# Two feature tiles of the expert stage lent to the weight stream as a ninth place

## The chip, the cores and the metric

The kernel runs on one core of a Trainium2 chip. The metric is the device time of one execution in microseconds (us). TensorE (PE) does the matmuls, ScalarE (ACT) and VectorE (DVE) do what stands between them, GpSimd (POOL) does little, and SyncE (SP) issues nearly all DMAs of weights from HBM into on-chip memory (SBUF).

## The reference, cut to what matters

Two layers over 256 tokens of width 1024. The even layer ends in a dense SwiGLU, the odd one in eight experts, of which each token uses two. Nearly three quarters of the time go into the experts:

```python
def swiglu(x, w_gate, w_up, w_down):
    return (jax.nn.silu(x @ w_gate) * (x @ w_up)) @ w_down

def moe_swiglu(x, router, w_gate, w_up, w_down):
    ...
    logits = (t @ router).astype(jnp.float32)
    top_logits, top_idx = lax.top_k(logits, TOP_K)
    ...
    for e in range(N_EXPERTS):
        out = out + gates[:, e:e + 1] * swiglu(t, w_gate[e], w_up[e], w_down[e])
    return out.reshape(bsz, s, d)
...
        x = layer_norm(ALPHA * x + moe_swiglu(x, router, w_gate, w_up, w_down), ln2_g, ln2_b)
```

Each expert has a gate and an up matrix of 1024 x 3584 and a down matrix of 3584 x 1024, all float32.

## The kernel before

**The pieces.** The experts' weights are 336 MB-sized pieces (`chunks`, filled by `expert`), here numbered 0 to 335 in the order in which they are used. `raw_half` gives each piece a place in SBUF (tile name `raw`) and issues its DMA at once (L136, 1 MB). A place is one of eight in the ring of the pool `rawp` (`RAW_BUFS`), or, for pieces 0 to 59, one of the extra places of `AHEAD`: fixed tiles of the pool `fx` (tags ft, fd, fa, ... f1) that stand empty for a while; each is open for a span of pieces. Which piece gets which place is worked out ahead of the program: a loop goes through the pieces and gives each the open place whose last piece is the oldest (`held_by`, result in `ahead`). A piece given a place waits until the place's last reader has read it.

**The order of work.** All DMAs of pieces are issued on SP's queue, in the order of the pieces. SP's queue is in order: while one DMA waits for its place, the ones behind it are not issued. What a piece waits for is a semaphore of PE or DVE, whichever read the old content last. A program-ordered plan (`plan`) lists, for every expert p and block of features f (`FBLOCKS`: 1024, 1024, 1024, 512), a gate item "g", an up item "u" and a down item "d"; a block of 1024 is four pieces. Experts are handled in places 0, 2, 6, 1, 4, 5, 3, 7, of which two or three overlap (`STARTS`). The items' instructions stand in this order on every engine.

**Wide and narrow experts.** `CAPS` gives the token slots of an expert. Blocks of 64 or 32 slots use the piece as it landed (PE reads `raw`). Experts 2, 1 and 3, in that order, have a 128-slot block: each half of a piece is first copied by ACT (`whi`, L154), then DVE makes the remainder (`wlo`, L161), and PE multiplies with both. Up to 6 `whi` and 5 `wlo` halves exist. Expert 1 has a block of 32 slots besides.

**The feature tiles.** The picked tokens of a 128-slot block (names `xgw`, `xgw2`, read by PE as `xgw`) lie in a tile of 128 x 8 x 256, the size of a piece. There are two in turn (`picked`): the pool `fx` has one under the tag f0 (experts 2 and 3), the pool `mop` one under the tag xgw (expert 1). Expert 0's 64-slot features (`xg`) use xgw as well, and at the very end the gains and biases of the last layer norm (`lnf`, 2 DMAs of 512 KB on POOL's queue, L1613) go into it. A block's features are picked by PE with a one-hot matrix S, made on DVE (L1214), and are last read by the last up matmul of their expert.

**Other names that come up.** `fdk` (L1339, L1352) are silu and product of a block, `mh` its transposed copy, `acc` the down accumulators. L1535 is a branch (`tc.If`) which all engines pass at about 1218 to 1234 us; SP reaches it after it has issued pieces up to 319, and goes on with piece 320 (a down piece of expert 3) behind it. L1655 and L1656 apply `lnf` in the last 5 us of work.

Of the kernel before, what the change touches and what calls it, by code (L numbers as in the profile page):

```python
# [8 lines left out]
F32 = mybir.dt.float32  # L9
# [8 lines left out]
P = 128  # L18
# [21 lines left out]
AHEAD = {"ft": (0, 50), "fd": (20, 24), "fa": (2, 17), "fc": (3, 48), "fe": (7, 50), "fb": (8, 56), "f0": (9, 16), "f1": (10, 60)}  # L40

IN_HI, IN_LO = (15, 16, 17), (18, 19)
# [18 lines left out]
FBLOCKS = ((0, 1024), (1024, 1024), (2048, 1024), (3072, 512))  # L61
# [17 lines left out]
def tile_trunk(ctx: ExitStack, tc: tile.TileContext, a: dict, out: bass.AP, caps=CAPS, starts=STARTS,  # L79
# [17 lines left out]
    def bank(tag="mm"):  # L97
        return psum.tile([P, 512], F32, name=tag, tag=tag)
# [5 lines left out]
    chunks, slot_pools = [], {"ra": rawp}  # L104
    raws, his, los, ahead = {}, {}, {}, {}
# [11 lines left out]
    def raw_half(n):  # L117

        c, h = divmod(n, 2)
        src, k, f = chunks[c]  # L120
        if c in ahead and ahead[c] in ("whi", "wlo"):
            if c not in raws:
                pool = hip if ahead[c] == "whi" else lop
                raws[c] = [pool.tile([P, k // 2, f], F32, name=ahead[c]) for _ in range(2)]
                for i, r in enumerate(raws[c]):
                    sy.dma_start(r, src()[:, i * k // 2:(i + 1) * k // 2, :])
            return raws[c][h]
        if c not in raws:
            tag = ahead.get(c, "raw")
            raws[c] = slot_pools[tag[:2]].tile([P, k, f], F32, name="raw", tag=tag)  # L130
            v = src()
            if c < FIRST_CUT:
                for i in range(2):
                    sy.dma_start(raws[c][:, :, i * P:(i + 1) * P], v[:, :, i * P:(i + 1) * P])
            elif c < len(chunks) - LAST_CUT:
                sy.dma_start(raws[c], v)  # L136
            else:
                for i in range(2):
                    sy.dma_start(raws[c][:, i * k // 2:(i + 1) * k // 2, :], v[:, i * k // 2:(i + 1) * k // 2, :])
        return raws[c][:, :, h * P:(h + 1) * P] if k == DB else raws[c][:, h * k // 2:(h + 1) * k // 2, :]  # L140
# [5 lines left out]
    def prep(hi_to, lo_to):  # L146
        hi_to, lo_to = (min(v, 2 * len(chunks) - 1) for v in (hi_to, lo_to))
        while made["hi"] <= hi_to:
            n = made["hi"]
            made["hi"] += 1  # L150
            r = raw_half(n)
            if n not in his and n not in plain:
                his[n] = hip.tile(list(r.shape), F32R, name="whi")
                se.activation(his[n], r, AF.Copy)  # L154
        while made["lo"] <= lo_to:
            n = made["lo"]
            made["lo"] += 1
            if n not in los and n not in plain:
                r = raw_half(n)
                los[n] = lop.tile(list(r.shape), F32R, name="wlo")  # L160
                ve.tensor_tensor(los[n], r, his[n].bitcast(F32), op=OP.subtract)  # L161
# [7 lines left out]
    def hold(n):  # L169

        r = raw_half(n)
        for d in (his, los):
            if n not in d:
                d[n] = spare_half().rearrange("p (k f) -> p k f", k=r.shape[1])
                if d is his:
                    se.activation(his[n], r, AF.Copy)
                else:
                    ve.tensor_tensor(los[n], r, his[n].bitcast(F32), op=OP.subtract)

    def use(count=1):  # L180

        n = state["use"]
        state["use"] = n + count
        if count == 1:
            end = n > 2 * len(chunks) - TAIL
            prep(n + (TAIL_HI if end else LOOK_HI), n + (TAIL_LO if end else LOOK_LO))
            return his.get(n), los.get(n)
        prep(n + count, n + count - 1)
        return [(his[m], los[m]) for m in range(n, n + count)]
# [38 lines left out]
    n_moe = 2 * len(chunks)  # L228
    NFB = len(FBLOCKS)

    held_by = {"raw": [-1] * 8}
    held_by.update({tag: [-2] for tag in AHEAD})
    for c in range(max(c1 for _, c1 in AHEAD.values())):
        if c in IN_HI + IN_LO:
            continue
        tag = min((v[0], t) for t, v in held_by.items() if t == "raw" or AHEAD[t][0] <= c < AHEAD[t][1])[1]
        held_by[tag] = held_by[tag][1:] + [c]  # L240
        if tag != "raw":
            ahead[n_moe // 2 + c] = tag
    passes = [[(p, n - n0) for p, n0 in starts if 0 <= n - n0 < NFB] for n in range(max(n0 for _, n0 in starts) + NFB)]
    plan = []
    for n, g in enumerate(passes):
# [8 lines left out]
    for p, n0 in sorted(starts, key=lambda s: s[1]):  # L254
        kept = [(m, k) for m, k in kept if m + NFB > n0]
        spills[p] = []
        for _, n in _blocks(caps[p]):
            k = 2 if n == P else 1
# [3 lines left out]
    if len(passes[-1]) == 1 and caps[last] < P:  # L262

        plan.insert(len(plan) - 2, plan.pop(len(plan) - 5))

    def expert(p, w, r0, nr, c0, ncol):
        def src():
            if p and p not in eid_reg:
                eid_reg[p] = sy.value_load(ctli[0:1, p:p + 1], min_val=0, max_val=NE - 1)
            if p == 0:  # L270
                v = w[0, r0:r0 + nr, c0:c0 + ncol]
            else:
                v = w[bass.ds(eid_reg[p], 1), r0:r0 + nr, c0:c0 + ncol].rearrange("o r f -> (o r) f")
            return v.rearrange("(k p) f -> p k f", p=P)
        chunks.append((src, nr // P, ncol))

    for what, p, f in plan:
        f0, nf = FBLOCKS[f]
# [121 lines left out]
    def ws_tile(w, xT, b=None, t=None):  # L400


        wh, wl = w
        if b is None:
            b = bank()
        o, ol = b, b[:, :T]
        if t is not None:
            o = ol = b.rearrange("p (s u f) -> p s u f", s=2, u=2)[:, :, t, :]
        for k in range(DB):
            x_, xl = xT[:, k, :], xT[:, k, :T]  # L410
            if t is not None:
                x_ = xl = x_.rearrange("p (s u f) -> p s u f", s=2, u=2)[:, :, t, :]
            if k < DB - 1:
                mm(o, wh[:, k, :], x_, k == 0, False)
                mm(ol, wl[:, k, :], xl, False, False)
            else:
                mm(ol, wl[:, k, :], xl, False, False)
                mm(o, wh[:, k, :], x_, False, True)
        return b
# [3 lines left out]
    def combine(b, o=None):  # L423
        c = evac[0][:, 1024 + T * (evac[1] % 2):][:, 0:T]
        se.activation(c, b[:, T:], AF.Copy)
        if o is None:
            o = evac[0][:, T * (evac[1] % 4):][:, 0:T]
        evac[1] += 1
        ve.tensor_tensor(o, b[:, :T], c, op=OP.add)
        return o  # L430
# [230 lines left out]
    def ws3(w):  # L661

        b = bank()
        for k in range(DB):
            mm(b[:, :T], w[0][:, k, :], xT[:, k, :T], k == 0, False)
            mm(b[:, :T], w[0][:, k, :], xT[:, k, T:], False, False)
        for k in range(DB):
            mm(b[:, :T], w[1][:, k, :], xT[:, k, :T], False, k == DB - 1)
        return b[:, :T]
# [42 lines left out]
    for pair in range(2):  # L712
        for h in range(2):
            s = ws3(use())
# [14 lines left out]
    for q in range(4):  # L729
        w = use_plain() if PLAIN_B else use()  # L730
        for t in range(2):
            for j in range(2):
                k = 2 * q + j
# [118 lines left out]
    first, firsts = [], []  # L852
# [22 lines left out]
    for i in range(1, NFP):  # L875
# [4 lines left out]
        b = [ws_tile(use(), x1T) for _ in range(2)]  # L880
# [30 lines left out]
    first, firsts = [], []  # L911
# [26 lines left out]
    b = bank()  # L938
# [6 lines left out]
    for pair in range(2):  # L945
        for h in range(2):
            w = use()
            j = 2 * pair + h
            s = combine(ws_tile(w, x2T))
# [7 lines left out]
    for n in range(2):  # L957
        b = bank()
        for h in range(4):
            mm(b[:, h * P:(h + 1) * P], vd[:, n, h * P:(h + 1) * P], swT[:, h, :], True, True)  # L960
        s = fc[:, 3, :]
# [7 lines left out]
    for pair in range(2):  # L969
        for h in range(2):  # L970
            w = use()
            j = 2 * pair + h
            s = combine(ws_tile(w, x2T))
# [7 lines left out]
    for pair in range(2):  # L981
        for h in range(2):
            w = use()
            j = 2 * pair + h
            s = combine(ws_tile(w, x2T))
# [68 lines left out]
    b = bank()  # L1054
# [21 lines left out]


    mop = ctx.enter_context(tc.tile_pool(name="mop", bufs=2, reuse_waits="tile"))
    events = {}
    clock = {"n": 0, "free": 0, "banks": 0}  # L1080

# [425 lines left out]
    at = len(plan)  # L1507
    for n, p in sorted([(plan.index(("g", p, 0)), p) for p, n0 in starts if n0], reverse=True):
        at = min(at, n - 1)
# [104 lines left out]
    for bi in range(len(blocks[last])):  # L1614
        if spills[last][bi]:
            spilled(last, NFB - 1, bi, macc[last, bi])
        else:
            n = len(macc[last, bi])
            ysum[last, bi] = [row0(i) for i in range(n)]
            if n == 1:  # L1620
                y, b = ysum[last, bi][0], macc[last, bi][0]
# [66 lines left out]
```

## Time and profile before

| | us |
|---|---|
| median of 3 runs | 1293.33 (1292.98 to 1293.68) |
| the profiled execution, its own time | 1298.7 |
| its span | 1297.0 |
| PE busy in it | 1248.3 (96%) |
| DVE busy / ACT busy | 711.9 / 515.4 |
| weights and the rest moved by DMA | 421.02 MB |
| pieces of 1 MB for the experts, issued on SP | 336 |

PE is busy nearly all the time, and so are the DMA engines in the last two thirds. With two resources so full, the rows to read are PE's few gaps and what ended each, and the stretches in which the DMA engines stand idle and what the next issue waited for. The clock of TensorE is in the rows as the granted share of full speed: 1.00 is 2.4 GHz, 0.50 is 1.2 GHz.

### The profile page before, as it was taken

What the parts mean: (1) busy time and instruction counts of PE and PEld (TensorE: products, weight loads), DVE (VectorE), ACT (ScalarE), POOL (GpSimd) and SP (SyncE); (2) the same over time, 40 slices, a digit from 0 to 9 for tenths busy, and PEclk for the clock granted to TensorE, in tenths of its full rate; (3) what the DMA queues carried; (4) which work ended last, traced back from release to release, by engine and by line L of the source; (5) the groups of instructions that cost most, each with busy time, mean ns of one, the idle gap of its engine ahead of it and who ended that gap; (6) DMA issues with size and microseconds to landing.
All of it is one profiled execution on the core that took longest, in us unless ns stands there. A gap on an engine that the chain in (4) does not pass through costs nothing. (4 is left out here: it accounts for less than half of the span.)

```text
span 1297.0 us, 17004 instructions
## 1 busy us (share of the span) xinstructions
PE 1248.3 (96%) x6433; PEld 803.9 (62%) x6433; DVE 711.9 (55%) x1066; ACT 515.4 (40%) x705; POOL 32.1 (2%) x69
## 2 busy tenths in 40 slices
PE   7989999999999999999999999999999999999795
PEld 7848888888876466855654455554454556765341
DVE  5997676667985247665234533534333575575233
ACT  4246555546432245554234332332221445454110
POOL 4000000001000001000000000000000000000000
PEclk9999999999999999999989999999999999999898
DMA  8425755176878999999969999899999999999995
GB/s 293 172 70 174 256 185 194 58 249 195 331 266 338 378 406 406 350 358 405 387 240 401 388 401 402 344 364 404 391 402 408 409 405 404 400 403 405 390 352 201
DMA packets 146642, 421.02 MB, mean 325 GB/s; under 512 B 6816, under 2 KB 43368, under 8 KB 146552
## 3 DMA queue, kind: packets, MB, share of 16 engines
q1 hardware_dynamic: 145048, 414.58, 84.0%
q0 software_dynamic: 1504, 5.28, 1.2%
q8 instruction: 52, 0.85, 0.3%
q14 instruction: 38, 0.31, 0.1%
HBM read 418.78 MB, written 1.05 MB: 324 GB/s over the span
## 5 line engine op out<-in xcount | busy, mean ns | idle before, releaser
L161 DVE TENSOR_TENSOR wlo<-raw,whi 128x1024 fp32r<-128x1024 f32 x354 | 419.1, 1225 | 200.8 <-ACT whi L154 169.8
L154 ACT ACTIVATE whi<-raw 128x1024 fp32r<-128x1024 f32 x354 | 357.6, 1052 | 218.3 <-DMA raw<-in_odd_moe_w_up 83.6
L101 PE MATMUL mm<-whi,xgw 128*128 128x512 f32 x672 | 216.6, 404 | 3.0 <-DVE total L1504 2.0
L101 PEld LDWEIGHTS mm<-whi,xgw 128*128 128x128 f32 x672 | 124.4, 191 | 48.1 <-issue 11.1
L101 PE MATMUL mm<-wlo,xgw 128*128 128x512 f32 x336 | 133.3, 397 | 0.5 <-DVE wlo L161 0.5
L101 PE MATMUL mm<-raw,f1k 128*64 128x512 f32 (+3 forms) x768 | 131.8, 552 | 0.0
L101 PE MATMUL mm<-big,whi 128*128 128x512 f32 (+1 forms) x448 | 129.7, 368 | 1.6 <-ACT whi L154 1.6
L101 PE MATMUL acc<-whi,mh 128*128 128x512 f32 (+1 forms) x352 | 111.7, 410 | 0.6 <-ACT whi L154 0.6
L101 PE MATMUL mm<-raw,fek 128*64 128x512 f32 (+1 forms) x512 | 103.3, 551 | 6.6 <-DVEq L1535 6.6
L101 PE MATMUL mm<-big,wlo 128*128 128x256 f32 x384 | 93.1, 284 | 0.0
L101 PE MATMUL acc<-raw,fbs 128*64 128x512 f32 (+1 forms) x560 | 91.5, 513 | 0.5 <-DMA raw<-in_odd_moe_w_down 0.5
L101 PEld LDWEIGHTS mm<-big,whi 128*128 128x128 f32 x448 | 75.5, 194 | 13.1 <-ACT whi L154 2.0
L101 PEld LDWEIGHTS mm<-raw,f1k 128*64 128x64 f32 (+1 forms) x768 | 40.6, 127 | 67.2 <-issue 59.9
L101 PEld LDWEIGHTS acc<-whi,mh 128*128 128x128 f32 (+1 forms) x352 | 62.5, 186 | 27.2 <-ACT whi L154 7.4
L101 PEld LDWEIGHTS mm<-raw,fek 128*64 128x64 f32 x512 | 35.3, 138 | 63.8 <-issue 58.7
L101 PEld LDWEIGHTS mm<-wlo,xgw 128*128 128x128 f32 x336 | 64.0, 191 | 15.5 <-DVE wlo L161 1.0
L1339 ACT ACTIVATE fdk<-mm 128x512 f32<-128x512 f32 (+1 forms) x37 | 21.1, 572 | 127.4 <-PE mm L101 126.7
L101 PEld LDWEIGHTS mm<-big,wlo 128*128 128x128 f32 x384 | 69.1, 191 | 3.6
L101 PE MATMUL acc<-wlo,mh 128*128 128x512 f32 (+1 forms) x184 | 70.2, 413 | 0.5 <-DVE wlo L161 0.5
L101 PEld LDWEIGHTS acc<-raw,fbs 128*64 128x64 f32 (+1 forms) x560 | 28.3, 125 | 53.2 <-issue 46.1
L1352 DVE TENSOR_TENSOR fdk<-mm,fdk 128x512 f32<-128x512 f32 (+1 forms) x37 | 24.4, 662 | 66.7 <-PE mm L101 66.7
L101 PE MATMUL acc<-whi,ffh 128*128 128x512 f32 x176 | 54.9, 393 | 0.0
(289 smaller groups left out, 1271.8 us busy)
## 6 DMA issues: line engine op xcount, KB each, us to landing
raw<-in_odd_moe_w_gate SPq DMA_DIRECT2D x112, 1024.0 KB, 11.5
raw<-in_odd_moe_w_up SPq DMA_DIRECT2D x111, 1024.0 KB, 11.4
raw<-in_odd_moe_w_down SPq DMA_DIRECT2D x106, 1024.0 KB, 11.9
raw<-in_even_ffn_w_gate SPq DMA_DIRECT2D x11, 1024.0 KB, 6.5
raw<-in_even_ffn_w_up SPq DMA_DIRECT2D x11, 1024.0 KB, 8.5
raw<-in_even_ffn_w_down SPq DMA_DIRECT2D x11, 1024.0 KB, 6.8
raw<-in_odd_w_in SPq DMA_DIRECT2D x10, 1024.0 KB, 14.7
raw<-in_even_w_in SPq DMA_DIRECT2D x5, 1024.0 KB, 9.0
```

The lines of the kernel that those rows point to most:

```text
L101: te.matmul(o, lhsT, rhs, start=start, stop=stop)
L154: se.activation(his[n], r, AF.Copy)
L161: ve.tensor_tensor(los[n], r, his[n].bitcast(F32), op=OP.subtract)
L1339: se.activation(s[:, n * i:n * (i + 1)], v, AF.Silu)
L1352: ve.tensor_tensor(s[:, c], v, s[:, c], op=OP.mult)
```

## The change

No computation is added or removed, and no engine's instructions change their order. What changes is the place of some pieces, and with it what they and the pieces behind them wait for. The loop over `held_by` moves behind the making of `plan` and goes through all pieces. Two tags get additional spans, worked out from the plan, in which they are open for pieces:

- xgw from piece 59 to 87 (after expert 0's last up item, until shortly before expert 1's features are picked): pieces 59, 68, 77, 86 get it;
- f0 from piece 101 to 219 (after expert 2's last up item, until shortly before expert 3's features are picked): 101, 110, ... 218;
- xgw again from 223 to 333 (after expert 1's last up item): 223, 232, ... 331.

Within a span the pieces go through nine places in turn, not eight, so that each one but the first takes the place of the piece nine before it. The first piece of a span takes a place that was a feature tile until then.

```diff
-            raws[c] = slot_pools[tag[:2]].tile([P, k, f], F32, name="raw", tag=tag)
+            raws[c] = slot_pools[tag[:2]].tile([P, k, f], F32, name="raw", tag=tag, **({"bufs": 1} if tag == "xgw" else {}))
...
-    for c in range(max(c1 for _, c1 in AHEAD.values())):
-        if c in IN_HI + IN_LO:
-            continue
-        tag = min((v[0], t) for t, v in held_by.items() if t == "raw" or AHEAD[t][0] <= c < AHEAD[t][1])[1]
...
+    at, spans = 0, {}
+    for item in plan:
+        spans[item] = at
+        at += FBLOCKS[item[2]][1] // 256
+    wides = [(p, n0) for p, n0 in sorted(starts, key=lambda s: s[1]) if caps[p] >= P]
+    free = {"f0": [], "xg": []}
+    firsts = {p: spans["g", p, 0] for p, _ in starts}
+    lasts = {p: spans["u", p, NFB - 1] + 2 for p, _ in starts}
+    free["f0"].append((lasts[wides[0][0]] + 3, firsts[wides[2][0]] - 10))
+    free["xg"].append((lasts[0] + 3, firsts[wides[1][0]] - 14))
+    free["xg"].append((lasts[wides[1][0]] + 3, at - 2))
+
+    def open_at(tag, c):
+        return tag in AHEAD and AHEAD[tag][0] <= c < AHEAD[tag][1] or any(a <= c < b for a, b in free.get(tag, ()))
+
+    held_by.setdefault("xg", [-2])
+    for c in range(at):
+        if c in IN_HI + IN_LO:
+            continue
+        tag = min((v[0], t) for t, v in held_by.items() if t == "raw" or open_at(t, c))[1]
+        held_by[tag] = held_by[tag][1:] + [c]
+        if tag != "raw":
+            ahead[n_moe // 2 + c] = {"xg": "xgw"}.get(tag, tag)
...
+    slot_pools["xg"] = mop
```

SP's queue at the start of the f0 span. The first row is piece 101 (expert 6, up), the next are pieces 102 to 104 (expert 1, gate), 105 and 106; a wait on PE_49 or DVE_49 is the wait for the place, DMAHW is the queue's own:

```order
 L136 DMA raw_5287<-in_odd_moe_w_up 128x2x1024 [waits DMAHW3_49,PE_49]
...
-L136 DMA raw_5301<-in_odd_moe_w_gate 128x2x1024 [waits DMAHW4_49,PE_49]
...
-L136 DMA raw_5322<-in_odd_moe_w_gate 128x2x1024 [waits DMAHW5_49,PE_49]
...
-L136 DMA raw_5340<-in_odd_moe_w_gate 128x2x1024 [waits DMAHW6_49,DVE_49]
...
+L136 DMA raw_5301<-in_odd_moe_w_gate 128x2x1024 [waits DMAHW4_49]
...
+L136 DMA raw_5322<-in_odd_moe_w_gate 128x2x1024 [waits DMAHW5_49]
...
+L136 DMA raw_5340<-in_odd_moe_w_gate 128x2x1024 [waits DMAHW6_49]
...
 L136 DMA raw_5388<-in_odd_moe_w_gate 128x2x1024 [waits DMAHW7_49,DVE_49]
...
-L136 DMA raw_5424<-in_odd_moe_w_gate 128x2x1024 [waits DMAHW0_49,PE_49]
...
+L136 DMA raw_5424<-in_odd_moe_w_gate 128x2x1024 [waits DMAHW0_49,DVE_49]
```

Nothing moved in place; the three pieces behind 101 have no wait for a place of their own any more, because 101's wait, in front of them, is for a later event than theirs would be. Pieces 60 (behind 59) and 224 to 227 (behind 223) lose theirs in the same way.

DVE's queue at the same place, the same before and after (the names raw_5301, raw_5322 and raw_5340 are pieces 102, 103 and 104):

```order
L441 TENSOR_TENSOR mh_5298<-mm_5291,mh_5298 128x4x128 [waits Activation_49]
L161 TENSOR_TENSOR wlo_5318<-raw_5301,whi_5312 128x1024 [waits DMAHW4_49,DVE_49,Activation_49]
L161 TENSOR_TENSOR wlo_5326<-raw_5301,whi_5316 128x1024 [waits DVE_49,Activation_49]
L161 TENSOR_TENSOR wlo_5332<-raw_5322,whi_5324 128x1024 [waits DMAHW5_49,DVE_49,Activation_49]
L1352 TENSOR_TENSOR fdk_4046<-mm_5281,fdk_4046 128x512 [waits PE_49]
L1214 TENSOR_SCALAR S_5337<-slot0_64_3355,valsP_3671 128x128 x2
L161 TENSOR_TENSOR wlo_5344<-raw_5322,whi_5330 128x1024 [waits DVE_49,Activation_49]
```

Nothing moved here: S for the picking of a block stands behind three remainders, of pieces 102 and 103.

POOL's queue at its end. The third span gives xgw to piece 331 last, so `lnf` waits behind it; in before it waits for expert 1's features:

```order
-L1613 DMA lnf<-in_odd_ln_g 128x1024 [waits DMASW3_49,DVE_49,PE_49]
-L1613 DMA lnf<-in_odd_ln_b 128x1024 [waits DMASW4_49]
...
+L1554 UNCONDITIONAL_BRANCH
+L1632 DMA lnf<-in_odd_ln_g 128x1024 [waits DMAHW3_49,DMAHW2_49,DMAHW4_49,DMAHW1_49,DMAHW5_49,DMAHW0_49,DMAHW6_49,DMASW3_49,DMAHW7_49,DVE_49,PE_49]
+L1632 DMA lnf<-in_odd_ln_b 128x1024 [waits DMASW4_49]
```

The two loads stand where they stood, and wait for the last reading of piece 331, and for hardware DMA queues besides.

## Rows read from the trace of the kernel before

**Rows 1.** The page, section 1: busy time by engine.

```profile
PE 1248.3 (96%) x6433; PEld 803.9 (62%) x6433; DVE 711.9 (55%) x1066; ACT 515.4 (40%) x705; POOL 32.1 (2%) x69
```

**Rows 2.** Stretches: length, busy by engine (count), granted clock, DMA share, GB/s.

```profile
840.00:850.00 10.00, 10.00 (x54) 5.59 (x52) 0.68 (x1) 2.34 (x5) 0.00 (x0) 1.00 0.67 218
950.00:960.00 10.00, 10.00 (x56) 5.86 (x57) 0.00 (x0) 0.00 (x0) 0.00 (x0) 1.00 1.03 410
654.40:661.20 6.80, 6.80 (x26) 4.44 (x26) 1.55 (x2) 0.64 (x2) 0.00 (x0) 0.50 0.89 313
1005.95:1009.36 3.41, 3.41 (x10) 2.63 (x9) 3.00 (x4) 3.34 (x5) 0.00 (x0) 0.50 1.03 410
1220.99:1227.80 6.81, 3.22 (x8) 1.12 (x10) 0.00 (x0) 0.00 (x0) 0.00 (x0) 0.50 1.02 396
```

**Rows 3.** Timeline of SP: start, length, issue of pieces 59 and 101.

```profile
512.65 0.37 SPq L136 DMA_DIRECT2D raw<-in_odd_moe_w_up  x1
630.85 0.37 SPq L136 DMA_DIRECT2D raw<-in_odd_moe_w_up  x1
```

**Rows 4.** Timeline of PE and ACT, 523 to 542 us; in brackets idle time and releaser.

```profile
523.93 3.67 PE L101 MATMUL mm<-raw,xg 128*64 128x256 f32 x32
531.25 1.05 ACT L154 ACTIVATE whi<-raw 128x1024 fp32r<-128x1024 f32 x1
541.33 1.06 ACT L154 ACTIVATE whi<-raw 128x1024 fp32r<-128x1024 f32 x1 [0.29 <-PE mm L101]
```

**Rows 5.** Timeline of PE, ACT and DVE, 643 to 654 us.

```profile
643.66 0.39 PE L101 MATMUL mm<-wlo,xgw 128*128 128x512 f32 x1
648.12 5.78 ACT L154 ACTIVATE whi<-raw 128x1024 fp32r<-128x1024 f32 x6
649.20 3.50 DVE L161 TENSOR_TENSOR wlo<-raw,whi 128x1024 fp32r<-128x1024 f32 x3 [0.25 <-ACT whi L154]
652.61 0.68 DVE L1352 TENSOR_TENSOR fdk<-mm,fdk 128x512 f32<-128x512 f32 x1
653.21 0.47 DVE L1214 TENSOR_SCALAR S<-slot,valsP 128x128 f32<-128x128 f32 x2
653.63 2.97 PE L101 MATMUL mm<-S,tok 128*128 128x64 f32 x16 [1.61 <-DVE S L1214]
```

**Rows 6.** Timeline of PE and ACT: expert 1's last up matmul, expert 3's first gate pieces.

```profile
976.90 0.40 PE L101 MATMUL mm<-wlo,xgw 128*128 128x512 f32 x1
1002.69 2.00 ACT L154 ACTIVATE whi<-raw 128x1024 fp32r<-128x1024 f32 x2 [10.65 <-DMA raw<-in_odd_moe_w_gate]
1003.80 0.73 PE L101 MATMUL mm<-whi,xgw 128*128 128x512 f32 x2 [0.99 <-ACT whi L154]
1005.06 0.50 PE L101 MATMUL mm<-wlo,xgw 128*128 128x512 f32 x1 [0.53 <-DVE wlo L161]
```

**Rows 7.** Timeline of PE behind the branch.

```profile
1224.58 15.54 PE L101 MATMUL mm<-raw,fek 128*64 128x512 f32 x64 [6.64 <-DVEq L1535]
1240.70 0.74 PE L101 MATMUL acc<-whi,mh 128*128 128x512 f32 x2 [0.58 <-ACT whi L154]
1241.96 0.50 PE L101 MATMUL acc<-wlo,mh 128*128 128x512 f32 x1 [0.52 <-DVE wlo L161]
```

**Rows 8.** The chain that ended last: start, length, what.

```profile
1234.38 5.12 DMA raw<-in_odd_moe_w_down
1239.59 1.06 ACT whi L154
1248.28 15.97 DMA raw<-in_odd_moe_w_down
1272.28 8.76 PE acc L101 x40
```

**Rows 9.** The tile lnf: its readers, its issue and the time to landing.

```profile
L1655 DVE SCALAR_TENSOR_TENSOR total<-total,ln_y,lnf x4: 743/746/752, 1288.1 to 1292.3; 128x512 f32<-128x512 f32 x4
L1613 POOL DMA_DIRECT2D lnf<-in_odd_ln_g x1: 585/585/585, 977.6 to 977.6; - x1
DMA to landing us min/median/max: 7.9/9.0/10.0
```

More of the change, by code (lines that the diff above doesn't have):

```diff
@@ L229, in tile_trunk @@
     NFB = len(FBLOCKS)
-    held_by = {"raw": [-1] * 8}
-    held_by.update({tag: [-2] for tag in AHEAD})
-    for c in range(max(c1 for _, c1 in AHEAD.values())):
-        if c in IN_HI + IN_LO:
-            continue
-        tag = min((v[0], t) for t, v in held_by.items() if t == "raw" or AHEAD[t][0] <= c < AHEAD[t][1])[1]
-        held_by[tag] = held_by[tag][1:] + [c]
-        if tag != "raw":
-            ahead[n_moe // 2 + c] = tag
     passes = [[(p, n - n0) for p, n0 in starts if 0 <= n - n0 < NFB] for n in range(max(n0 for _, n0 in starts) + NFB)]
@@ L264, in tile_trunk @@
         plan.insert(len(plan) - 2, plan.pop(len(plan) - 5))
+    held_by = {"raw": [-1] * 8}
+    held_by.update({tag: [-2] for tag in AHEAD})
+    at, spans = 0, {}
[19 more added lines that the diff above has]
+            ahead[n_moe // 2 + c] = {"xg": "xgw"}.get(tag, tag)
     def expert(p, w, r0, nr, c0, ncol):
```

## The prediction

> **What bounds the kernel now.** I read the page first. PE is busy for 96% of the span [rows 1], so in the expert part a change of waits can win only what PE still idles, plus what low clock those idle times bring. Then the stretches by clock and DMA: where the stream of pieces runs freely the DMA engines are full, 410 GB/s at a share of 1.03 [rows 2], and a piece of 1.05 MB takes 1.05/0.410 = 2.56 us. At 840 to 850 us the share is 0.67: all places are taken there and the DMA engines wait for PE [rows 2]. So the two are nearly level: PE sets the pace over long stretches, and the stream is late at single points.
>
> Last, PE's gaps in its timeline, with what ended each. Three could depend on weights. At 652.02 PE waits 1.61 us for S [rows 5], and then runs at half clock (0.50, 1.2 GHz) from 654.40 to 661.20 [rows 2]. At 1002.8 and 1004.5 it waits 0.99 us for `whi` and 0.53 us for `wlo`; ACT had been idle 10.65 us, and a DMA of a gate piece ended that [rows 6]; the clock is 0.50 from 1005.95 to 1009.36 [rows 2]. Behind the branch it waits 0.58 and 0.52 us [rows 7], where SP issues the first piece at 1234.38 and the chain of waits gives it 5.12 us to land [rows 8]. The branch itself, 6.64 us [rows 7], is no weight's. The end is a chain of late DMAs and PE: a down piece issued at 1248.28 lands 15.97 us later [rows 8].
>
> **The steady part, priced at nothing.** Inside a span each piece takes the place of the piece nine before it, so its wait ends one piece earlier. Where the DMA engines are full, an earlier issue only lengthens the queue. It buys one piece of lead, 2.56 us, to be spent where PE would wait for a landing. In a full stretch such as 950 to 960 PE is busy 10.00 of 10.00 us [rows 2], so nothing is bought there.
>
> **The first piece of each span** is another matter: it takes a feature tile, and waits for the last matmul that reads it. SP's queue is in order, so everything behind it is held. Three such entries.
>
> *Piece 59* was issued at 512.65 [rows 3]. The matmuls that read expert 0's features run from 523.93 for 3.67 us [rows 4], so it can go at 527.6, and lands 5.1 to 5.3 us on, at some 533. ACT's copy of its first half started at 531.25 [rows 4], so it is late by under 2 us, and pieces 60 to 63, at 2.56 us each, land at 535.5, 538.1, 540.6 and 543.2. ACT is ahead of PE there: at 541.33 it had waited 0.29 us for PE to free a `whi` [rows 4], and so again before the three copies behind. Narrow pieces follow, read later still. I price it at 0. If that cover is less than it looks, it costs up to 1.5 us.
>
> *Piece 101* was issued at 630.85 [rows 3]. Expert 2's last up matmul ends at 643.66 + 0.39 = 644.05 [rows 5], 13.2 us later. Nothing is issued in those 13 us, so I take the queue as empty by then, and 101 lands 5.12 us on [rows 8], at 649.2; 102 at 651.8, 103 at 654.3. They are wide, and DVE's order puts S behind three remainders, the third from piece 103. Before, ACT started on 102 at 648.12 and S started at 653.21 [rows 5]. Now ACT starts on 103 at 654.3 or 654.4, its remainder starts 1.08 us later (648.12 to 649.20), lasts 3.50/3 = 1.17; then `fdk` 0.60 (652.61 to 653.21) and S 0.42 to PE's start at 653.63 [rows 5]. 654.4 + 1.08 + 1.17 + 0.60 + 0.42 = 657.7. PE starts 4.1 us later than before: **+4.1**, bounds 3.8 and 4.5 by the latencies.
>
> The half clock behind that wait changes too. Before, PE worked through all 6.80 us of it, which costs 3.4. The nearest row for a wait of 5.7 us is the branch: 6.64 us idle, half clock from 1220.99 for 6.81 us, with only 3.22 us of PE work in it [rows 2, 7], so a cost of 1.6. I take that row: **-1.8**, bounds -1.8 and 0 (where the low stretch starts as late after the wait as before).
>
> The Trainium skill (DMA: Bandwidth & Descriptors, "Anatomy of one DMA — SWDGE (gpsimd) path") says that DMA engines do not wait on semaphores: every wait happens on the issuing sequencer ahead of dispatch. By that the pieces behind a waiting one are all held, as I have it; if the engines did the waiting, 102 and 103 would be issued at their old times and the 4.1 would be gone. The trace agrees as far as it goes: the row of 101's issue [rows 3] comes 0.37 us long at its release, with no later piece issued ahead of it; no row here shows the other case.
>
> *Piece 223* waits for expert 1's last up matmul, 976.90 + 0.40 = 977.3 [rows 6], about 10 us later than before. It lands 5.12 to 5.3 us on, at 982.5, and the pieces follow at 2.56: piece 230, expert 3's first gate piece, at 982.5 + 7 x 2.56 = 1000.4. In before it came at 1002.6, just ahead of ACT's start at 1002.69 [rows 6]. That seems strange for a wait that begins later. It comes about since the two `lnf` loads, issued from 977.6 and landing in 7.9 and 10.0 us [rows 9], no longer share the engines there: 1.05 MB, 2.56 us. With `whi` 2.2 us earlier, both waits of PE go, 0.99 + 0.53 [rows 6]: **-1.5**; and the half clock behind them, 3.41/2 [rows 2]: **-1.7**. Bounds: both stay (0), or both go (-3.2).
>
> **The branch.** SP passes it when its pieces have landed, and starts the stream anew. The stream came 2.2 us nearer, PE 3.2 us, so the first pieces behind the branch are later against PE by 1.0: its waits there, 0.58 + 0.52 [rows 7], grow by **+1.0** (bounds 0 and 1.5).
>
> **The last layer norm.** `lnf` now waits until PE has read piece 331, in the last 40 matmuls from 1272.28 on [rows 8], at 8 a piece up to about 1274. It is needed at 1288.1 [rows 9]: 14 us, against 7.9 to 10.0 for a load in a full queue [rows 9]. So it is in time, but shares the engines with the last three or four pieces. All of it in front of the last landing would cost 2.56 us, none 0. I take **+1.0**, since its first 3 us or so pass before bytes move and the stream then has some 3 us left.
>
> **The sum.** 4.1 - 1.8 - 1.5 - 1.7 + 1.0 + 1.0 = +1.1 us. The profiled execution would go from 1298.7 (span 1297.0) to 1299.8; I put the same difference on the median of the unprofiled runs, 1293.33, which is 5.4 us below the profiled time, so that small waits may differ in them: **1294.5 us**.
>
> **Rivals.**
>
> *The entries are not paid back (slower).* The mechanism is piece 101's wait on SP: 4.1 us of PE time that no later row gives back, if the wait at 1002.8 is not there in unprofiled runs, or if piece 230 comes no earlier than before since 223's own late landing (982.5) eats what `lnf` left. Then 4.1 - 1.8 + 1.0 (`lnf`) = +3.3, and with the half clock as long as before +5.1: 1296.6 to 1298.4. It decides from the point where piece 230 lands less than 1 us earlier against PE than before. For it: the stall at 652 follows from a chain of rows without slack; its repayment needs three rows to come out as I read them. Against: the `lnf` load does leave the place where PE waits for a landing.
>
> *The lead is worth more (faster).* The entry at 101 could be hidden, if PE reads S before it needs piece 103, or if the wait ends on an earlier reader. Then 1.6 + 3.4 us around 652 stay as they are, and the gains at 1002.8 (3.2) and, with 2.56 us more lead behind the branch, 1.1 + 0.5 there come in full: -4.8, 1288.5. The skill's Trainium Kernel Development and Optimization, Best Practices, holds that buffering overlaps DMA with compute; by that alone a ninth place gains. In this trace it could gain where PE waits for a landing, and those rows are the ones just named, so it is this rival and no other. Against it: DVE's order has S behind the three remainders.
>
> *Nothing moves.* PE sets the pace and all three entries are covered by pieces already landed: 1293.3. Against it: 101 to 103 have to land before S, and 8 pieces of lead cannot cover 13.2 us of silence, since from 644 on PE reads the last of them, expert 6's up pieces. It falls into the same range of times as the forecast.
>
> *lnf comes too late.* If it takes over 14 us from its release, the last multiplications at 1288.1 wait, by the excess. Loads of 10.0 us in a full queue and an emptying queue speak against it; worth +1 to +4, and inside the slower case.
>
> **How the numbers follow.** A measurement of this kernel can tell about 0.2%, 2.6 us, from no change: below 1290.7 is faster, above 1295.9 slower. Forecast and the rival of no change together 0.51, nearly all of it within 0.2%; the entries not paid back 0.35, `lnf` late 0.04, both slower; the lead worth more 0.10, faster. Low end: half clock at its smaller cost, gains in full, nothing for `lnf` or the branch: 4.1 - 1.8 - 3.2 = -0.9, and 1.4 more towards the faster rival, 1291.0. High end: the unpaid case with its clock, 1298.4, and a part of a late `lnf`: 1299.0.
>
> **What would show it.** In the changed kernel's trace: SP's issue of 101 at about 644, not 631; PE's wait for S at 652 grown from 1.6 to 5 or 6 us, with half clock that begins inside it; no wait of PE at the first wide gate pieces of expert 3 (1003 plus the shift), and full clock behind; `lnf` issued near 1275, and DMA engines with a second gap at about 980. I would be wrong if PE's wait for S did not grow, or if the waits at expert 3's gate stayed. The single number that decides is PE's shift at its first matmul behind the 1003 wait: forecast +2.3 before that wait, -0.9 behind it.

## The result, and the profile of the changed kernel

| | median us | lowest to highest | runs |
|---|---|---|---|
| before | 1293.15 | 1291.44 to 1293.79 | 6 |
| changed | 1301.65 | 1299.73 to 1303.89 | 6 |

The ratio is 1.0064, with a 95% interval of 1.0053 to 1.0075: slower by 0.64%, some 8.3 us. On another chip, beside the variants below, it was 1.0065 (1.0050 to 1.0081). The forecast was no change at 1294.5, the range ended at 1299.0, so the time lies outside it. In the experiments below, one execution of 1785.38 us, of the twelve with f0 late, counts in no ratio.

The two profiled executions differ by much less: spans of 1300.4 and 1297.0 us, +3.4. The profiled execution of before was 5.5 us over the median of its kernel, that of the changed kernel 0.4 over its own. That difference turns out to be half of the story.

PE, ACT and DVE of the changed kernel at its three critical places: the wait for S, expert 3's first gate pieces, and the stretch behind the branch (start, length, operation; in brackets the idle time and what ended it). They answer to [rows 5], [rows 6] and [rows 7]:

```profile
653.14 2.00 ACT L154 ACTIVATE whi<-raw 128x1024 fp32r<-128x1024 f32 x2 [5.01 <-DMA raw<-in_odd_moe_w_gate]
655.70 2.00 ACT L154 ACTIVATE whi<-raw 128x1024 fp32r<-128x1024 f32 x2 [0.56 <-DMA raw<-in_odd_moe_w_gate]
656.79 1.22 DVE L161 TENSOR_TENSOR wlo<-raw,whi 128x1024 fp32r<-128x1024 f32 x1 [0.20 <-ACT whi L154]
657.93 0.68 DVE L1371 TENSOR_TENSOR fdk<-mm,fdk 128x512 f32<-128x512 f32 x1
658.53 0.47 DVE L1233 TENSOR_SCALAR S<-slot,valsP 128x128 f32<-128x128 f32 x2
658.96 3.65 PE L101 MATMUL mm<-S,tok 128*128 128x64 f32 x16 [7.02 <-DVE S L1233]
...
1006.63 0.73 PE L101 MATMUL mm<-whi,xgw 128*128 128x512 f32 x2
1007.51 0.50 PE L101 MATMUL mm<-wlo,xgw 128*128 128x512 f32 x1
...
1226.77 15.94 PE L101 MATMUL mm<-raw,fek 128*64 128x512 f32 x64 [6.70 <-DVEq L1554]
1243.65 0.72 PE L101 MATMUL acc<-whi,mh 128*128 128x512 f32 x2 [0.94 <-ACT whi L154]
1244.91 0.50 PE L101 MATMUL acc<-wlo,mh 128*128 128x512 f32 x1 [0.54 <-DVE wlo L161]
```

PE's wait for S has grown from 1.61 to 7.02 us. ACT is idle 5.01 us until piece 102 lands, and the chain behind it is the one in DVE's order: remainder, `fdk`, S. PE's shift against before can be read off row by row: 658.96 - 653.63 = 5.3 us at S, 1006.63 - 1003.80 = 2.8 at the first wide gate matmul of expert 3, where the wait of 0.99 is gone, 2.2 behind the branch, 2.95 at the first down matmul there. Between S and expert 3 it rises to 6.2 in the half clock behind S, falls by 1.6 at 828, where before's trace has 3.41 us of half clock and this one none, and by 0.7 at 710. There PE waits for DVE's `total`, which stands behind three remainders as S does; the prediction did not list this among the gaps that depend on weights. Before, then changed:

```profile
710.85 0.72 PE L101 MATMUL mm<-whi,xgw 128*128 128x512 f32 x2 [2.01 <-DVE total L1504]
...
716.30 0.74 PE L101 MATMUL mm<-whi,xgw 128*128 128x512 f32 x2 [1.29 <-DVE total L1523]
```

SP's issues of pieces 57 to 62, 101 and after, and 223 to 225 (start, length), which answer to [rows 3]; in the first row three issues stand together, the last of them, 59, ends at 507.42 + 20.52 = 527.94, where 527.6 was forecast:

```profile
507.42 20.52 SPq L136 DMA_DIRECT2D raw<-in_odd_moe_w_up  x3
528.14 1.69 SPq L136 DMA_DIRECT2D raw<-in_odd_moe_w_gate  x3
...
644.00 0.37 SPq L136 DMA_DIRECT2D raw<-in_odd_moe_w_up  x1
645.20 19.70 SPq L136 DMA_DIRECT2D raw<-in_odd_moe_w_gate  x10
...
981.21 2.92 SPq L136 DMA_DIRECT2D raw<-in_odd_moe_w_up  x3
```

Piece 101 goes at 644.00 and not at 630.85, as forecast, and 102 another 1.20 us later. Granted clock and DMA in three stretches (length, busy of PE, PEld, DVE, ACT, POOL with counts, clock, DMA share, GB/s), to be held against [rows 2]:

```profile
657.37:667.61 10.24, 8.65 (x32) 6.25 (x33) 4.09 (x7) 3.39 (x5) 0.00 (x0) 0.50 1.03 410
1003.00:1013.00 10.00, 9.67 (x42) 5.39 (x39) 5.83 (x5) 6.47 (x7) 0.00 (x0) 1.00 1.02 408
977.00:987.00 10.00, 10.00 (x74) 6.48 (x75) 2.35 (x6) 0.98 (x2) 0.00 (x0) 1.00 0.53 188
```

Half clock lasts 10.24 us, with 8.65 us of PE work in it, where before had 6.80. At expert 3's gate pieces the clock is full. At piece 223's entry the DMA engines stand idle for about half of 10 us, (1.03 - 0.53) x 10 / 1.03 = 4.9 us. And the last layer norm's load, to [rows 9]:

```profile
L1674 DVE SCALAR_TENSOR_TENSOR total<-total,ln_y,lnf x4: 743/744/753, 1291.5 to 1295.6; 128x512 f32<-128x512 f32 x4
L1632 POOL DMA_DIRECT2D lnf<-in_odd_ln_g x1: 587/587/587, 1277.3 to 1277.3; - x1
DMA to landing us min/median/max: 6.4/6.7/7.0
```

It lands by 1285 and is wanted at 1291.5.

Every sign that the prediction named is there: the late issue of 101, the long wait for S with half clock that begins inside it, no wait at expert 3's first gate pieces and full clock behind, `lnf` issued at 1277, a second gap of the DMA engines at 980. The time is wrong all the same.

### The profile page after: what moved, and what is told of

Same layout as the page of the kernel before. It is cut to its first block, busy times and chain, and to the rows that moved or that the text cites. A ratio compares the mean times of both kernels' runs of the same rounds, so it can differ in the third digit from the quotient of the medians.

```text
span 1300.4 us, 17000 instructions
## 1 busy us (share of the span) xinstructions
PE 1245.0 (96%) x6433; PEld 800.7 (62%) x6433; DVE 711.3 (55%) x1066; ACT 514.8 (40%) x705; POOL 32.6 (3%) x69
```

## The experiments

All are variants of a few lines, each timed in turns with before on the same chip; the ratio is to before. They ran in three groups on three chips: up to all three entries late; up to f0 late; the last four. Where ratios of two groups are subtracted, the result is good to about 0.2%.

### The kernel before, once more

> The kernel before, unchanged, to see how far its trace and its times repeat. Theory A (the waits at expert 3's first gate pieces, 0.99 + 0.53 us and 3.41 us of half clock, are a matter of one execution and absent in the others): the new trace has a span of some 1291 to 1293 us and no wait over 0.3 us there. Theory B (they are in every execution, and the profiled execution of before was longer for another reason): the waits stand there again and the span is about 1297 us. Ratio to before 1.000 in both.

Ratio 1.0004 (0.9990 to 1.0019). Over the three groups the executions of before, these among them, ran from 1289.86 to 1299.33 us. Its new trace has a span of 1294.6, and at expert 3's gate pieces, against [rows 6]:

```profile
1002.03 0.73 PE L101 MATMUL mm<-whi,xgw 128*128 128x512 f32 x2
1003.29 0.50 PE L101 MATMUL mm<-wlo,xgw 128*128 128x512 f32 x1 [0.53 <-DVE wlo L161]
```

The wait of 0.99 us is 0.14 here (PE's previous matmul ends at 1001.90), that for `wlo` is 0.53 again, and the half clock at 1006 is absent; the one behind S lasts 3.41 us, not 6.83, and there is one of 3.41 at 711 that the first trace has not. So neither theory holds in full: part of the wait is in both traces, but most of what I counted as waiting to be won, and above all its half clock, is in one of the two.

PE ahead of and behind expert 3's first gate pieces, in the changed kernel, in before, and in this trace:

```profile
1001.60 0.66 PE L1382 MATMUL mm<-ident,fdk 128*128 128x128 f32 x4
1040.13 0.70 PE L101 MATMUL mm<-fcs,fek 32*128 32x256 f32 x4
...
997.71 0.66 PE L1363 MATMUL mm<-ident,fdk 128*128 128x128 f32 x4
1038.85 0.70 PE L101 MATMUL mm<-fcs,fek 32*128 32x256 f32 x4
...
996.80 0.66 PE L1363 MATMUL mm<-ident,fdk 128*128 128x128 f32 x4
1035.45 0.70 PE L101 MATMUL mm<-fcs,fek 32*128 32x256 f32 x4
```

Against the first trace the changed kernel's PE is 3.9 us behind, then 1.3: most of the loss is paid back. Against the second it is 4.8 and 4.7 behind: next to nothing is.

### Only the span of f0

```diff
-    free["xg"].append((lasts[0] + 3, firsts[wides[1][0]] - 14))
-    free["xg"].append((lasts[wides[1][0]] + 3, at - 2))
```

> Only the span of f0 (pieces 101 to 218) is opened, both spans of xgw stay shut; lnf loads where it did before. Theory A (piece 101's wait on SP costs it all): PE waits about 7 us for S at 652, as in the changed kernel, and the time is +7 to +8.5 us, about 1300.5 to 1301.5. Theory B (the three entries share the cost): +2 to +4 us, the rest lies with pieces 59 and 223 and lnf.

Ratio 1.0035 (1.0024 to 1.0046). PE waits 6.88 us for S, and half clock lasts 13.65 us with 8.81 us of work in it:

```profile
655.02:668.67 13.65, 8.81 (x32) 6.38 (x33) 7.19 (x9) 6.25 (x8) 0.00 (x0) 0.50 1.03 412
```

The loss at S is all there, and yet the kernel loses only about half as much as the change. Theory A misses: piece 101 does not carry the whole net loss. Theory B is nearer, though 0.35% is 4.5 us and its range ended at 4: the xgw spans add to the loss.

### Only the spans of xgw

```diff
-    free["f0"].append((lasts[wides[0][0]] + 3, firsts[wides[2][0]] - 10))
```

> The counterpart: both spans of xgw are opened (59 to 87, 223 to 333), f0 stays shut. Theory A: PE waits 1.6 us for S at 652 as before, and the time is within 1.5 us of before. Theory B: +3 to +5 us, from piece 223's entry and from lnf in the tail.

Ratio 1.0001 (0.9991 to 1.0011), the wait for S 1.61 us. As theory A has it, by itself. Taken with the last run, 0.35% and 0.01% do not add up to 0.64%: the two spans get in each other's way. DMA around piece 223:

```profile
972.00:982.00 10.00, 9.91 (x75) 5.98 (x75) 3.90 (x9) 0.98 (x2) 0.00 (x0) 1.00 0.85 312
```

The hole at piece 223 is (1.03 - 0.85) x 10 / 1.03 = 1.7 us here, and 4.9 in the change.

### All three entries late

```diff
-    free["f0"].append((lasts[wides[0][0]] + 3, firsts[wides[2][0]] - 10))
-    free["xg"].append((lasts[0] + 3, firsts[wides[1][0]] - 14))
-    free["xg"].append((lasts[wides[1][0]] + 3, at - 2))
+    free["f0"].append((lasts[wides[0][0]] + 8, firsts[wides[2][0]] - 10))
+    free["xg"].append((lasts[0] + 7, firsts[wides[1][0]] - 14))
+    free["xg"].append((lasts[wides[1][0]] + 7, at - 2))
```

> All three spans, but each opened at the piece that would be issued about when the feature tile comes free: 63 (instead of 59), 106 (instead of 101), 227 (instead of 223). No piece waits longer for its place than before. Theory A: the wait at 652 is 1.6 us again and the time is within 1 us of before, or up to 3 us below it where the waits at expert 3's gate pieces are real. Theory B (a ninth place itself harms, by lnf in the tail or by a DMA queue that is fuller): still +3 us or more.

Ratio 0.9960 (0.9947 to 0.9974), 1290.13 us: faster than both. What PE waits for behind 600 us (engine, operation, what it waited for: us in total, times, longest):

```profile
PE mm L101 <- DVEq L1554: 6.6, 1, 6.6
PE mm L101 <- DVE S L1233: 2.7, 2, 1.6
PE mm L101 <- DVE total L1523: 1.3, 1, 1.3
PE mm L1382 <- ACT f1k L1215: 0.9, 2, 0.5
PE mm L1382 <- DVE fdk L1371: 0.8, 1, 0.8
PE mm L101 <- ACT fdk L1641: 0.7, 1, 0.7
PE acc L101 <- DMA raw<-in_odd_moe_w_down: 0.2, 1, 0.2
```

No wait for `whi` or `wlo` is left. The ninth place is worth something; the change loses it, and more, by when it opens it. Theory A, and somewhat beyond its 3 us.

### The change, once more

> The changed kernel once more, beside the variants on the same chip. +7 to +8.5 us against before, PE's wait for S about 7.0 us, half clock of 7 to 14 us behind it. If instead the time were below +5 us, the first comparison would have been a matter of the chip.

Ratio 1.0065 (1.0050 to 1.0081), 1302.64 against 1293.58 us. PE waits 6.85 us for S, half clock lasts 13.66 us:

```profile
652.58:666.24 13.66, 8.88 (x32) 6.48 (x33) 7.26 (x9) 6.26 (x8) 0.00 (x0) 0.50 1.03 410
```

### The expert's number loaded earlier

In the order of SP a register load stands between pieces 101 and 102, which I had shown but not priced. Here it stands with expert 6's.

```diff
-            if p and p not in eid_reg:
-                eid_reg[p] = sy.value_load(ctli[0:1, p:p + 1], min_val=0, max_val=NE - 1)
+            for q in (p, {6: 1}.get(p, p)):
+                if q and q not in eid_reg:
+                    eid_reg[q] = sy.value_load(ctli[0:1, q:q + 1], min_val=0, max_val=NE - 1)
```

> The change with one edit: SP loads the number of expert 1 into its register where it loads that of expert 6, not between the issues of pieces 101 and 102. Theory A (the load stretches the first issue to 1.20 us in an empty queue, and the landing of 102 with it): 102 lands 2.56 us behind 101, not 3.75, PE's wait for S falls from 7.0 to 5.8 us, the time by 1 to 2 us against the change. Theory B (the second piece into an empty queue lands late whatever SP does): step and wait stay as they were.

Ratio 1.0060 (1.0046 to 1.0074), the wait for S 6.94 us. SP's issues, and ACT's start on 102:

```profile
643.98 0.37 SPq L136 DMA_DIRECT2D raw<-in_odd_moe_w_up  x1
644.58 2.51 SPq L136 DMA_DIRECT2D raw<-in_odd_moe_w_gate  x4
...
653.05 2.00 ACT L154 ACTIVATE whi<-raw 128x1024 fp32r<-128x1024 f32 x2 [4.93 <-DMA raw<-in_odd_moe_w_gate]
```

102 is issued 0.60 us behind 101 and lands as late as before, 3.8 us behind it. Theory A falls: the load is not what delays 102. Why this step is 3.8 us and not 2.56 stays open; the last section has a candidate.

### f0 opened one piece later

```diff
-    free["f0"].append((lasts[wides[0][0]] + 3, firsts[wides[2][0]] - 10))
+    free["f0"].append((lasts[wides[0][0]] + 4, firsts[wides[2][0]] - 10))
```

> The change with the span of f0 opened one piece later: 101 goes into the ring and is issued at 631, 102 waits for the feature tile. Theory A (the stall is the chain landing of 103, copy, remainder, fdk, S): 102 lands at 649.3, 103 at 651.8, S about 2.5 to 3.7 us earlier than in the change, PE's wait 3.3 to 4.5 us, not 7.0; the time 3 to 5 us below the change. Theory B (the loss is the empty DMA queue as such, 8 us of it): the time stays within 1.5 us of the change, since the queue is empty as long.

Ratio 1.0039 (1.0025 to 1.0053), 4.1 us under the change. The wait for S and the rows ahead of it:

```profile
651.09 2.00 ACT L154 ACTIVATE whi<-raw 128x1024 fp32r<-128x1024 f32 x2 [1.62 <-DMA raw<-in_odd_moe_w_gate]
652.17 1.23 DVE L161 TENSOR_TENSOR wlo<-raw,whi 128x1024 fp32r<-128x1024 f32 x1 [1.26 <-ACT whi L154]
653.32 0.68 DVE L1371 TENSOR_TENSOR fdk<-mm,fdk 128x512 f32<-128x512 f32 x1
654.34 1.88 PE L101 MATMUL mm<-S,tok 128*128 128x64 f32 x8 [4.51 <-DVE S L1233]
```

One wide piece less behind the waiting one, and the wait falls by 2.5 us (2.3 against the change's 6.85 on this chip), where a piece takes 2.56. The chain from 103's landing to S is what sets PE's start: theory A.

### f0 late, xgw as in the change

```diff
-    free["f0"].append((lasts[wides[0][0]] + 3, firsts[wides[2][0]] - 10))
+    free["f0"].append((lasts[wides[0][0]] + 8, firsts[wides[2][0]] - 10))
```

> The change with the span of f0 opened at 106, and the entries of xgw at 59 and 223 as in the change. Theory A (piece 101 carries the loss, the other two entries are nearly free): PE's wait for S is 1.6 us, the time -3 to -4.5 us against before, as with all three entries late. Theory B (piece 223's entry and lnf cost as well): about 2 us behind the kernel with all three late, so -2.5 us against before.

Ratio 1.0011 (1.0000 to 1.0023), 8.1 us below the change on the same chip (7.0 by the ratios), and 0.5% above all three late. The wait for S is 1.61 us; but the later waits are back, 0.97 + 0.52 us behind the branch. DMA around piece 223:

```profile
968.00:978.00 10.00, 10.00 (x75) 6.64 (x75) 2.14 (x5) 0.98 (x2) 0.00 (x0) 1.00 0.55 199
```

The hole is (1.03 - 0.55) x 10 / 1.03 = 4.7 us, as in the change. So the entries at 59 and 223 together are not free: theory B, and more than it said.

### S made earlier, in the change

```diff
+    onehot, NEXT_ONEHOT = {}, {(1, 1): (4, 0), (4, 0): (5, 0)}
...
-        S = mop.tile([P, 2, P], F32, name="S", bufs=2)
+        S = onehot.pop((p, bi), None) or make_onehot(p, bi)
+        if (p, bi) in NEXT_ONEHOT:
+            onehot[NEXT_ONEHOT[p, bi]] = make_onehot(*NEXT_ONEHOT[p, bi])
```

> The change, with the one-hot matrix S of expert 4's block made on DVE one gathering earlier, ahead of the three remainders of pieces 102 and 103 (and that of expert 5 likewise). Theory A (piece 101 costs time since S stands behind those remainders): PE's wait for S of 7.0 us is gone or under 0.3 us; a wait for copies or remainders of 102 and 103 of 1 to 2.5 us takes its place some 3 us later; the time falls by 4 to 7 us against the change, to +2 to +4 us against before. Theory B (PE is short of the pieces 102 to 105 themselves): the wait only moves to the wide matmuls, 5 us or more of it, and the time falls by under 2 us.

Ratio 0.9990 (0.9974 to 1.0005): some 0.75%, over 9 us, below the change, though nothing was done to piece 101. PE's rows, with no wait for S any more:

```profile
651.76 2.00 PE L101 MATMUL mm<-S,tok 128*128 128x64 f32 x16
653.68 1.07 PE L101 MATMUL mm<-raw,f1k 128*32 128x512 f32 x8
654.68 0.72 PE L101 MATMUL mm<-whi,xgw 128*128 128x512 f32 x2
655.25 0.49 PE L101 MATMUL mm<-wlo,xgw 128*128 128x512 f32 x1
658.41 1.22 PE L101 MATMUL mm<-whi,xgw 128*128 128x512 f32 x2 [2.67 <-DVE fdk L1380]
```

The pieces come as late as in the change, and PE waits 2.67 us for `fdk`, which stands behind the same remainders, instead of 7.02 for S. Theory A, with a somewhat longer wait and a larger gain than it said. The gain is larger than the 4.4 us of this wait and the 1.08 us of S at 825 together; its profiled execution, of 1296.7 us span, still has 13.65 us of half clock and lies at the slow end of this kernel's runs (1290.5 to 1298.8), so what makes up the rest is not shown.

### S made earlier, and all three entries late

The two edits together.

> All three spans opened late (63, 106, 227) and both S made earlier. Theory A: the waits of 1.61 and 1.08 us for S go, with them what half clock they start; 2 to 4 us below the kernel with all three late, about -6 to -8 us against before. If PE were held by pieces there, the waits would turn up a few us later and the time would be that of all three late, -4.5 us.

Ratio 0.9925 (0.9905 to 0.9946), 1286.16 us: 0.75% below before and the fastest of all. Its list of waits is that of the kernel with all late, without the row for S, and PE's clock is full from 600 us to the branch. Theory A: it is 0.35% below all three late, some 4.5 us, of which the two waits are 2.7.

### Only 59 early

```diff
-    free["f0"].append((lasts[wides[0][0]] + 3, firsts[wides[2][0]] - 10))
-    free["xg"].append((lasts[wides[1][0]] + 3, at - 2))
+    free["f0"].append((lasts[wides[0][0]] + 8, firsts[wides[2][0]] - 10))
+    free["xg"].append((lasts[wides[1][0]] + 7, at - 2))
```

> Spans opened at 59 (as in the change), 106 and 227. With 59, 106 and 223 the time was level with before; with 63, 106 and 227 it was -4.5 us. Theory A (piece 223's wait costs the difference, since the stream is full from there to the branch): about -4 us, no waits over 0.3 us at expert 3's gate pieces and behind the branch. Theory B (piece 59's costs it): within 1 us of before.

Ratio 0.9967 (0.9953 to 0.9982). Against all late (0.9960) the entry at 59 costs nothing that the intervals show; against f0 late (1.0011) the entry at 223 costs 0.44%, some 5.7 us. DMA around the same piece:

```profile
968.00:978.00 10.00, 10.00 (x75) 6.17 (x73) 2.75 (x7) 0.98 (x2) 0.00 (x0) 1.00 1.03 407
```

Here the engines stay full, and no wait for `whi` or `wlo` is left at expert 3's gate pieces or behind the branch. Theory A.

### No third span

All late, without the line for xgw after expert 1.

> Spans at 63 and 106 only; xgw stays shut after expert 1, so lnf loads from 977 as in before. Theory A (the third span gives the lead for expert 3's gate pieces, and moves lnf out of a full stream): 2 to 3 us behind all three late, so about -2 us against before, with a wait of PE at expert 3's gate pieces or behind the branch. Theory B (the lead of f0 is enough): as all three late, -4.5 us.

Ratio 0.9950 (0.9930 to 0.9970). As all three late: theory B. One of A's signs is there, waits of 0.14 and 0.53 us behind the branch, but none at expert 3's gate pieces. Within the intervals, of 0.2%, the third span brings nothing, and `lnf` costs nothing in either place.

## Why the prediction was wrong

In the terms of the sum: the wait put at +4.1 was +5.4, the half clock behind it put at -1.8 was +0.9, the payback of -3.2 was read from one execution and is not there in the second, the entry at 223 was costed only through that payback and costs 5.7 us, and the steady part, put at nothing, brings 5.2.

By ratios against before, 0.1% being 1.3 us, the change is made of four parts: the ninth place with no entry that waits, -0.40% (all late); the entry at 59, +0.07% (only 59 early less all late), inside the intervals; the entry at 223, +0.44%; the entry at 101, 1.0065 - 1.0011 = +0.54%. They add up to the change's +0.65%, as they must, being differences of one row of kernels. In us: -5.2, +0.9, +5.7, +7.0, each of the last three good to 2.5 us. They hold for this order: only f0 less no third span gives 0.35 + 0.50 = 0.85%, 11 us, for the entry at 101 where no entry at 223 follows (the first of the two has no span of xgw at all). So the two entries seem to spend in part the same lead.

**The steady part** was priced at nothing, with 2.56 us of lead to be spent where PE waits for a landing. It is worth 5.2 us. The rival of a faster kernel had the right places and -4.8 as its price; it needed late entries to come true. The waits it named, 0.67 us at expert 3's gate pieces and 0.65 behind the branch in the second trace of before, are gone in the trace of all late; so is part of the one at 710, which was 2.01 and 1.78 us in the two traces of before, 1.85 with only xgw's spans, and 1.29 in every kernel with f0's. Two stretches of half clock that the second trace of before has, at 656 and 711, are gone too; whether the ninth place took them away is not shown.

**The entry at 59** was priced at 0: right, within 0.2%.

**The entry at 101**: the mechanism, DVE's order with S behind three remainders, was right. Moving S takes the wait away, and one piece less behind 101 takes 2.3 to 2.5 us of it. The size was off twice. First the wait: +4.1 forecast, 7.02 - 1.61 = 5.4 measured. I had 102 landing 2.56 us behind 101, and it came 3.8 us behind; ACT began on it at 653.14, not 651.8. That 1.2 to 1.3 us is the whole difference between the two waits. The register load that I suspected is not its cause. Second the half clock behind the wait: -1.8 forecast, on the row of the branch, with bounds -1.8 and 0. Measured against before's trace it is 8.65/2 = 4.3 in place of 3.4, so +0.9, beyond the bound. The four traces with a wait of 6.85 to 7.02 us all have 8.5 to 8.9 us of work at half clock. The branch row had a low stretch that began early in its idle time; here it began later, or lasted longer. This was the step that failed worst in the forecast of the profiled execution.

**The payback at 1002.8**, -1.5 and -1.7: in the profiled execution it came nearly as forecast. PE's shift was to fall from 2.3 to -0.9 there and falls from 3.9 to 1.3 us, the clock is full from 1003 to 1013, and 230's copy starts 1005.14 against 1002.69, so earlier against PE. But it was counted against [rows 6] of one execution, 5.4 us over the median. The second trace of before has a wait of 0.14 + 0.53 and no half clock there, and against it PE's shift stays at 4.8 to 4.7; before's profiled execution also had the full 6.83 us of half clock behind S and 3.41 us more at 828, while six traces with the same 1.61 us wait for S had none or 3.41 behind it. I wrote that small waits may differ in the unprofiled runs and then put the whole difference on the median. That was the decisive step: the -3.2 was put on the median, and there it is not to be had. The profile gave +3.4, the medians +8.5; the 5 us between them are by how much further this one execution of before lay above its median than that of the changed kernel. Which of its rows the other executions lacked is shown by the second trace alone. Low clock has a part in the medians too: beside the variants the changed kernel's six executions had a mean granted clock of 0.986, before's seventeen 0.989, which is 0.003 x 1300 = 3.9 us at most (half clock while PE waits costs nothing).

**The entry at 223** was counted as a gain, since `lnf` leaves the stream. The wait of 10 us on SP was costed only against the one place where PE waited. It empties the DMA engines for 4.9 us in a stretch where they are otherwise full, about what the lead of the ninth place (2.56) and the bytes of `lnf` (2.56) come to together; that they are what is spent is a reckoning, not shown. With f0's span it costs 5.7 us (f0 late against only 59 early), with a hole of 4.7 us; without f0 the hole is 1.7 us and xgw's spans are level (1.0001). That fits the two parts that did not add up. Back in f0 late's trace are the waits behind the branch, 0.97 + 0.52, as in the change.

**The branch**, +1.0: 0.94 + 0.54 against 0.58 + 0.52, +0.4. **lnf**, +1.0: it was issued at 1277.3; near the end PE has one wait more, of 0.27 us, whose cause is not shown, and the kernel without the third span shows no difference. Both over-priced.

**The rivals.** "The entries are not paid back" was the right one: its condition, that the wait at 1002.8 is not there in other executions, held for the one other that was traced, in the main. Its price, 3.3 to 5.1, was short by the same two terms as the forecast (1.3 of wait, 0.9 and up of clock against a trace that itself was slow there) and by 223's entry. The trace agrees with the rule of the Trainium skill (DMA: Bandwidth & Descriptors, "Anatomy of one DMA — SWDGE (gpsimd) path") that waits are held on the issuing sequencer: 102 and the pieces after it were issued from 645.20 on, behind 101, though by the order 102 to 104 wait for no place of their own.

## What to carry to other kernels

A new buffer in an in-order queue of loads must be free by the time its first load would go anyway; open it a few pieces later rather than as early as it is allowed, since one waiting load holds all the loads behind it, and in a full stream the hole stays: the one of 4.7 us at piece 223 cost 5.7. Price the wait at every place behind it that reads from the stream, and in every engine's order, not only at the gap that caught the eye. Look also at what small, ready work stands in an engine's order behind work that waits for loads: moving one such instruction ahead took away a wait of 7 us. And do not count as gain what one profiled execution shows when that execution is longer than the median by more than the effect: look at a second trace of the kernel before.

## What the runs showed of the hardware

The same wait of 1.61 us for S was followed by 6.83 us of half clock in the first trace of before, 3.41 in the second and with no third span, and none in four others (only xgw, all late, f0 late, only 59 early). A wait of 4.51 us came with 6.83, one of 2.67 us with 13.65 (12.27 of it with matmuls running), and those around 7 us with 10.24 to 13.66. So the half clock behind the same 1.61 us cost between 0 and 3.4 us of PE time from trace to trace, and behind the 2.67 us 6.1. The executions of before spread by 9 us on one chip; the longest of these, 1299.08 us, had a mean granted clock of 0.984, the shortest, 1290.12, of 0.991, and 0.007 x 1295 is 9 us as well.

A piece issued into an empty queue landed 5.0 to 5.5 us later at the entries of 59 and 101, and 5.8 to 6.8 at that of 223; the next one 3.6 to 3.8 us behind it at the entry of f0 (in five kernels), but 2.6 us behind it at 59's and 223's. What makes the difference was not found. A candidate is in the traces: in all six with this step (the change was traced twice) one load of instructions, 16 KB, starts within 1 us of the landing of the piece that waited. In the changed kernel it takes 0.015 x 16 x 4 = 0.96 us of one engine's time; DMA from 646 to 650 (queue, kind: packets, MB, share of 16 engines):

```profile
q1 hardware_dynamic: 390, 1.53, 97.1%
q8 instruction: 1, 0.02, 1.5%
```

With f0 late such a load passes at the same place without a longer step, so that it is the cause is not shown.
